# Side work at every fourth weight tile, and an early function table, in a mixture-of-experts loop

## The chip, the core and the metric

The kernel runs on one core of a Trainium2 chip. The core's engines run side by side and wait for one another by semaphores: TensorE (PE; its weight loads are shown apart as PEld), VectorE (DVE), ScalarE (ACT), GpSimd (POOL), and SyncE (SP), which here only issues transfers. Sixteen DMA engines move data. The metric is the device time of one execution in microseconds; lower is better.

## The reference

One transformer layer over 1024 tokens of width 1024: three kinds of attention side by side, an output projection, and a mixture of 32 experts, of which each token takes two; then a norm. The part that matters here is the mixture. Each expert's tokens go through two weight matrices (1024x1024 up, 512x1024 down); the result is scaled by the token's gate and added up per token:

```python
dest = pad_start[e_sorted] + jnp.arange(n_assign) - start[e_sorted]
buf = jnp.zeros((n_blocks * MOE_BLOCK, D), h.dtype).at[dest].set(h[tok_sorted])
...
def expert_block(args):
    xb, e = args
    g, u = jnp.split(xb @ w_up[e], 2, axis=-1)
    return (jax.nn.silu(g) * u) @ w_down[e]
...
y = y[dest] * gate.reshape(-1)[order][:, None].astype(h.dtype)
return jax.ops.segment_sum(y, tok_sorted, num_segments=n_tok)
```

## The kernel before, in words

The attention and the routing come first. The expert stage follows, some 650 us of the run. It gives each expert one block of 128 token slots. Tokens beyond an expert's 128 go to overflow blocks, which run in a second loop at the very end, under an If that is taken only where there are any.

**The main loop.** It walks 360 weight tiles of 128x1024 float32 (512 KB each) of 30 experts, eight tiles of the up matrix (kind 0) and four of the down matrix (kind 1) each. The down block of an expert stands behind the up block of the next one, so that twelve tiles make one expert's turn. The remaining two experts are done behind the loop, together with the final norm. For each tile j the loop writes, in this order:

- turns that are due (`e_turn`, line 1856): PE transposes of a 128x512 half of the next expert's gathered rows `xg` (the two halves at the second and third tile of a down block) or of the hidden rows `sg` (at the fifth tile of an up block) into a PSUM tile `ept`. ACT copies that tile out (`xh` or `ah`, line 1858), then DVE subtracts this from it (`xl` or `al`, line 1859), and the tile is free after that;
- `e_mm` (lines 1866 to 1868): six matmuls with the high and low pieces of tile j into `epu` (up) or `epy` (down);
- one step of the side work, if any is left;
- at the end of an up block `e_silu`: ACT's Silu and DVE's product (`sg`, lines 1872 and 1873);
- `split_next(j + 3)`: ACT rounds a later tile to `whi` (line 1840), DVE takes the rest `wlo` (line 1841); there are three such pairs of buffers. The raw buffer in the ring of 34 is then free, and SP issues the load of tile j + 37;
- at the end of a down block `e_scatter`: half of the scaled result `y` by ACT, half by DVE (line 1892), and POOL adds it to memory (line 1886).

The order on PE, DVE, ACT and POOL is that of the code (a manual schedule); the tile framework puts in the semaphores and picks a free buffer.

**The side work.** `overflow_tables` is a generator that builds the tables of the overflow blocks, about 60 steps of mostly one DVE instruction. It begins at tile 52. Its first 26 steps are small tables (lines 1740 to 1797). Then it takes a PSUM tile for itself, `ptab`, and from there on makes 16 pairs of one-hot matrices (`ohr` and `ohc`, lines 1809 and 1811, a step each) and adds their 16 products up in `ptab` on PE (line 1805), each product two pairs behind its matrices. A last pair of steps reads `ptab`. `ptab` comes from the pool that the turns use, under the same name, and that pool has two buffers of it:

```python
pe = Ex.enter_context(tc.tile_pool(name="pe", bufs=2, space=PSUM))
pt = pe.tile([128, 4, 128], F32, name="ept")      # in e_turn
ptab = pe.tile([128, 4, 128], F32, name="ept")    # in overflow_tables
```

**The start of the stage.** `gates()` computes the gates with two Exp on ACT (lines 1706 and 1710). Then the first expert's two halves are turned. POOL sets six small tiles `gxs` to zero ahead of it (line 2046). ACT can use a function only while the table that holds it is loaded; where the next function needs another table, an ACT_TABLE_LOAD stands ahead of it. Exp and Silu need different ones here; the copies do not.

Of the kernel before, what the change touches and what calls it, by code (L numbers as in the profile page):

```python
# [12 lines left out]
AF = mybir.ActivationFunctionType  # L13
# [53 lines left out]
def body(nc, tc, d, tap=None, upto=None):  # L67
# [1238 lines left out]
    class Til:  # L1306
# [5 lines left out]
        def small(self, name, shape, bufs=2):  # L1312
            return w2.tile([128] + shape, F32, name=name, bufs=bufs)
# [387 lines left out]
    def gates():  # L1701

        ge = rt_("ge", [NT, 4])
        V.tensor_tensor(ge, lg[:, :, 0:4], bc(gmx[:, :, 0], 4), op=OP.subtract)
        yield
        nc.scalar.activation(ge, ge, AF.Exp)
        dd = rt_("dd", [NT])
        V.tensor_sub(dd, gmx[:, :, 2], gmx[:, :, 1])
        yield
        nc.scalar.activation(dd, dd, AF.Exp)  # L1710
        pg = rt_("pg", [NT])
        V.tensor_reduce(pg, ge, axis=AX.X, op=OP.add)
        yield
        V.reciprocal(pg, pg)
        yield
        ds_ = rt_("ds", [NT])
        V.tensor_scalar(ds_, dd, 1.0, None, op0=OP.add)
        yield
        V.reciprocal(ds_, ds_)
        yield  # L1720
        V.tensor_mul(gate[:, 0, :], ds_, pg)
        yield
        V.tensor_mul(ds_, ds_, dd)
        yield
        V.tensor_mul(gate[:, 1, :], ds_, pg)
        yield
        gd = [rt_(f"gd{j}", [NT, E]) for j in range(2)]
        for j in range(2):
            V.tensor_tensor(gd[j], cio99[:, None, :].to_broadcast([128, NT, E]), bc(eid[:, j, :], E), op=OP.is_equal)
            yield  # L1730
            V.tensor_tensor(gd[j], gd[j], bc(gate[:, j, :], E), op=OP.mult)
            yield
        V.tensor_add(gd[0], gd[0], gd[1])
        nc.gpsimd.dma_start(GD.rearrange("(t p) e -> p t e", p=128), gd[0])
        yield
# [113 lines left out]
    def x_tiles():  # L1849
        return (e2.tile([128, 8, 128], F32R, name="xh", bufs=1), e2.tile([128, 8, 128], F32R, name="xl", bufs=1))  # L1850

    def e_turn(src, n, h, l, g):

        pt = pe.tile([128, 4, 128], F32, name="ept")
        for i in range(4):
            nc.tensor.transpose(pt[:, i, :], src[:, (4 * g + i) * 128:(4 * g + i + 1) * 128], ident)  # L1856
        gs = slice(4 * g, 4 * g + 4)
        nc.scalar.copy(h[:, gs, :], pt)  # L1858
        nc.vector.tensor_sub(l[:, gs, :], pt, h[:, gs, :].bitcast(F32))  # L1859

    def e_mm(ps, k, nk, w, a):
        hi, lo = w
        ah, al = a
        for n in range(2):
            cs = slice(512 * n, 512 * n + 512)
            nc.tensor.matmul(ps[:, cs], lhsT=ah[:, k, :], rhs=hi[:, cs], start=(k == 0), stop=False)  # L1866
            nc.tensor.matmul(ps[:, cs], lhsT=ah[:, k, :], rhs=lo[:, cs], start=False, stop=False)  # L1867
            nc.tensor.matmul(ps[:, cs], lhsT=al[:, k, :], rhs=hi[:, cs], start=False, stop=(k == nk - 1))  # L1868

    def e_silu(pu):  # L1870
        sg = e2.tile([128, 512], F32, name="sg", bufs=1)
        nc.scalar.activation(sg, pu[:, 0:512], AF.Silu)
        nc.vector.tensor_mul(sg, sg, pu[:, 512:])
        return sg

    def a_tiles():
        return (e2.tile([128, 4, 128], F32R, name="ah", bufs=1), e2.tile([128, 4, 128], F32R, name="al", bufs=1))
# [11 lines left out]
    def e_scatter(py, gi_, g_):  # L1889
        y = e2.tile([128, D], F32, name="y", bufs=2)  # L1890
        nc.scalar.activation(y[:, :HD], py[:, :HD], AF.Copy, scale=g_)
        V.scalar_tensor_tensor(y[:, HD:], py[:, HD:], g_, m5[:, HD:], op0=OP.mult, op1=OP.mult)  # L1892
        y_scatter(y, gi_)
# [19 lines left out]
    def split_next(j):  # L1913
        if j < NM:
            pieces[j] = split(loaded.pop(j))
            if j + RW < len(stream):
                load_tile(j + RW)
            else:
                fill()
# [24 lines left out]
    gxs = [small(f"gx{i}", [E]) for i in range(6)]  # L1944
# [6 lines left out]
    def gate_of(e):  # L1951
        return gxs[e % 6][:, e:e + 1]

    def gather(e):
        e_gather(gU[:, e:e + 1], xgs[e % 2])
        gate_rows(gU[:, e:e + 1], gxs[e % 6])
# [43 lines left out]
    def turn32(src, n, dst, g):  # L2000

        pt = pe.tile([128, 4, 128], F32, name="ept")
        for i in range(4):
            nc.tensor.transpose(pt[:, i, :], src[:, (4 * g + i) * 128:(4 * g + i + 1) * 128], ident)
        (nc.vector.tensor_copy if g else nc.scalar.copy)(dst[:, 4 * g:4 * g + 4, :], pt)
# [15 lines left out]
    with tc.manual_schedule(engines={ET.PE, ET.DVE, ET.Activation, ET.Pool}):  # L2021
# [24 lines left out]
            nc.gpsimd.memset(g_, 0.0)  # L2046
        for _ in gates():
            pass
        e_turn(xgs[0], 8, *xs[0], 0)
        e_turn(xgs[0], 8, *xs[0], 1)  # L2050
        for j in range(1, SP):
# [8 lines left out]
        side_work = iter(())  # L2060
        ps = None
        for j, (b, k) in enumerate(stream[:NM]):
            kind, e = blocks[b]
            for what, e_, g in extra.get(j, ()):
                if what == "h":
                    acts[e_] = a_tiles()
                    e_turn(sgs.pop(e_), 4, *acts[e_], 0)
                else:
                    if e_ >= ME:
                        if e_ == ME and g == 0:  # L2070
                            xs[ME], xs[E - 1] = (a.bitcast(F32) for a in x_tiles())
                        turn32(xgs[e_ % 2], 8, xs[e_], g)
                    else:
                        if g == 0:
                            xs[e_] = x_tiles()
                        e_turn(xgs[e_ % 2], 8, *xs[e_], g)
                    if g == 1 and e_ + 2 < E:
                        gather(e_ + 2)
            if k == 0:
                ps = (pe.tile([128, D], F32, name="epu"), None)[0] if kind == 0 else pd.tile([128, D], F32, name="epy")  # L2080
            e_mm(ps, k, (8, 4)[kind], pieces.pop(j), xs[e] if kind == 0 else acts[e])
            if (b, k) == (8, 0):
                side_work = overflow_tables(cid2)
            next(side_work, None)
            if kind == 0 and k == 7:
                sgs[e] = e_silu(ps)
            split_next(j + SP)
            if kind == 1 and k == 3:
                e_scatter(ps, gU[:, e:e + 1], gate_of(e))
# [283 lines left out]
```

## Time and profile before

| | us |
|---|---|
| median of 3 runs (1587.26 to 1592.28) | 1589.0 |
| the profiled execution, its own time | 1589.09 |
| its span, first to last instruction | 1587.3 |
| PE busy | 1447.1 (91%) |
| DVE busy | 1144.6 (72%) |
| ACT busy | 947.5 (60%) |

The profile comes from one execution. 1.8 us of its time lie outside the span. A share of busy time is an average over stages with different limits: in the expert loop PE, DVE and the DMA engines are each near their limit, in the stages before it they are not.

### The profile page before, as it was taken

What the parts mean: (1) busy time and instruction counts of PE and PEld (TensorE: products, weight loads), DVE (VectorE), ACT (ScalarE), POOL (GpSimd) and SP (SyncE); (2) the same over time, 40 slices, a digit from 0 to 9 for tenths busy, and PEclk for the clock granted to TensorE, in tenths of its full rate; (3) what the DMA queues carried; (4) which work ended last, traced back from release to release, by engine and by line L of the source; (5) the groups of instructions that cost most, each with busy time, mean ns of one, the idle gap of its engine ahead of it and who ended that gap; (6) DMA issues with size and microseconds to landing.
All of it is one profiled execution on the core that took longest, in us unless ns stands there. A gap on an engine that the chain in (4) does not pass through costs nothing. (4 is left out here: it accounts for less than half of the span.)

```text
span 1587.3 us, 24530 instructions
## 1 busy us (share of the span) xinstructions
PE 1447.1 (91%) x8577; PEld 1182.9 (75%) x8577; DVE 1144.6 (72%) x1929; ACT 947.5 (60%) x1544; POOL 486.9 (31%) x611
## 2 busy tenths in 40 slices
PE   6899799888999989699999859999999999999993
PEld 3699677767767867689999857877788888888751
DVE  6613655894545436586777768999999999999936
ACT  3523554773534441477766427877788888888721
POOL 0001333221313211347788653232222222222101
PEclk9999899999989979799999979999999999999997
DMA  9433563014554369522222678999999999999994
GB/s 333 142 88 117 163 223 119 21 48 144 132 134 111 74 222 300 212 74 67 87 67 67 246 269 320 363 348 343 335 371 369 357 364 358 364 354 363 360 333 158
DMA packets 166272, 354.11 MB, mean 223 GB/s; under 512 B 29407, under 2 KB 85194, under 8 KB 166144
## 3 DMA queue, kind: packets, MB, share of 16 engines
q1 hardware_dynamic: 139552, 305.68, 54.5%
q0 software_dynamic: 22992, 36.76, 9.0%
q10 hardware_dynamic: 3600, 10.06, 1.6%
q8 instruction: 68, 1.11, 0.3%
q14 instruction: 60, 0.49, 0.1%
HBM read 315.68 MB, written 55.72 MB: 234 GB/s over the span
## 5 line engine op out<-in xcount | busy, mean ns | idle before, releaser
L1841 DVE TENSOR_TENSOR wlo<-wraw,whi 128x1024 fp32r<-128x1024 f32 x360 | 435.7, 1221 | 31.7 <-ACT whi L1840 27.8
L1840 ACT CAST whi<-wraw 128x1024 fp32r<-128x1024 f32 x360 | 374.9, 1049 | 107.9 <-PE epu L1868 65.4
L1866 PE MATMUL epu<-whi,xh 128*128 128x512 f32 x480 | 195.0, 406 | 2.2 <-ACT xh L1858 2.2
L1867 PE MATMUL epu<-wlo,xh 128*128 128x512 f32 x480 | 191.8, 400 | 1.9 <-DVE wlo L1841 1.8
L1868 PE MATMUL epu<-whi,xl 128*128 128x512 f32 x480 | 190.1, 396 | 0.4 <-DVE xl L1859 0.4
L1270 DVE TENSOR_REDUCE nm<-S 128x1 f32<-128x1280 f32 x64 | 94.9, 1489 | 51.0 <-PE S L1269 43.3
L1845 POOL DMA_INDIRECT xg<-H,gidx x30 | 31.9, 1064 | 294.3 <-PE ept L1856 294.0
L377 PE MATMUL pj<-wh,hh 128*128 128x256 f32 (+1 forms) x384 | 113.8, 296 | 3.1 <-ACT kbT L333 3.1
L379 PE MATMUL pj<-wh,hl 128*128 128x256 f32 (+1 forms) x384 | 112.4, 293 | 0.0
L378 PE MATMUL pj<-wl,hh 128*128 128x256 f32 (+1 forms) x384 | 112.3, 292 | 0.0
L1867 PEld LDWEIGHTS epu<-wlo,xh 128*128 128x128 f32 x480 | 90.8, 189 | 28.1 <-DVE wlo L1841 9.6
L1866 PEld LDWEIGHTS epu<-whi,xh 128*128 128x128 f32 x480 | 90.9, 189 | 22.4 <-ACT xh L1858 2.7
L1868 PEld LDWEIGHTS epu<-whi,xl 128*128 128x128 f32 x480 | 90.7, 189 | 22.3 <-DVE xl L1859 1.3
L1886 POOL DMA_INDIRECT YS<-y,gidx x30 | 71.1, 2369 | 115.0 <-DVE y L1892 96.4
L1866 PE MATMUL epy<-whi,ah 128*128 128x512 f32 x240 | 101.1, 421 | 3.3 <-DVE y L1892 3.3
L366 PE MATMUL pj<-hh,wh 128*128 128x512 f32 (+1 forms) x240 | 99.7, 416 | 0.0
L1275 ACT ACTIVATE p<-S,nm 128x1280 f32<-128x1280 f32 x64 | 84.7, 1331 | 21.2 <-DVE nm L1270 21.2
L1867 PE MATMUL epy<-wlo,ah 128*128 128x512 f32 x240 | 95.3, 397 | 0.1
L1868 PE MATMUL epy<-whi,al 128*128 128x512 f32 x240 | 94.9, 395 | 0.0
L368 PE MATMUL pj<-hh,wl 128*128 128x512 f32 (+1 forms) x240 | 92.3, 385 | 0.0
L367 PE MATMUL pj<-hl,wh 128*128 128x512 f32 (+1 forms) x240 | 92.1, 384 | 0.0
L1268 PE MATMUL S<-ak,aq 128*128 128x512 f32 (+1 forms) x192 | 75.4, 393 | 10.8 <-ACT p L1275 10.0
(493 smaller groups left out, 3479.7 us busy)
## 6 DMA issues: line engine op xcount, KB each, us to landing
wraw<-w_up SPq DMA_DIRECT2D x254, 512.0 KB
wraw<-w_down SPq DMA_DIRECT2D x127, 512.0 KB
wm<-w_mod SPq DMA_DIRECT2D x32, 512.0 KB
raw<-w_in SPq DMA_DIRECT2D x22, 512.0 KB
wm<-w_mod SPq DMA_DIRECT2D x32, 256.0 KB
aq<-QS SPq DMA_DIRECT2D x64, 128.0 KB
ak<-KS SPq DMA_DIRECT2D x8, 640.0 KB
xn<-x SPq DMA_DIRECT2D x8, 512.0 KB
```

The lines of the kernel that those rows point to most:

```text
L366: nc.tensor.matmul(ps[:, :n], lhsT=a, rhs=x, start=(k == 0), stop=False)
L367: nc.tensor.matmul(ps[:, :n], lhsT=a, rhs=y, start=False, stop=False)
L368: nc.tensor.matmul(ps[:, :n], lhsT=b, rhs=x, start=False, stop=(k == 7))
L377: nc.tensor.matmul(ps[:, :n], lhsT=a, rhs=wh[:, k, :], start=(k == 0), stop=False)
L378: nc.tensor.matmul(ps[:, :n], lhsT=a, rhs=wl[:, k, :], start=False, stop=False)
L379: nc.tensor.matmul(ps[:, :n], lhsT=b, rhs=wh[:, k, :], start=False, stop=(k == 7))
L1270: V.tensor_reduce(u.nm[:, m:m + 1], sv, axis=AX.X, op=OP.max, negate=True)
L1840: nc.scalar.copy(hi, raw)
L1841: nc.vector.tensor_sub(lo, raw, hi.bitcast(F32))
L1866: nc.tensor.matmul(ps[:, cs], lhsT=ah[:, k, :], rhs=hi[:, cs], start=(k == 0), stop=False)
L1867: nc.tensor.matmul(ps[:, cs], lhsT=ah[:, k, :], rhs=lo[:, cs], start=False, stop=False)
L1868: nc.tensor.matmul(ps[:, cs], lhsT=al[:, k, :], rhs=hi[:, cs], start=False, stop=(k == nk - 1))
```

## The change

The side work advances at every fourth tile of the loop and not at every tile, and ACT runs a Silu over one column of zeros ahead of the first expert's turns.

```diff
         for _ in gates():
             pass
+
+        nc.scalar.activation(gxs[5][:, 0:1], gxs[5][:, 0:1], AF.Silu)
         e_turn(xgs[0], 8, *xs[0], 0)
         e_turn(xgs[0], 8, *xs[0], 1)
...
             e_mm(ps, k, (8, 4)[kind], pieces.pop(j), xs[e] if kind == 0 else acts[e])
             if (b, k) == (8, 0):
                 side_work = overflow_tables(cid2)
-            next(side_work, None)
+            if j % 4 == 0:
+                next(side_work, None)
```

On ACT the table load moves. Before, it stands ahead of the first expert's Silu (line 1872; `m` and `cid` are loads that ACT only issues):

```order
L1710 ACTIVATE dd<-dd 128x8 [waits DVE_49]
L1858 CAST xh<-ept 128x512 [waits PE_49] x2
L1840 CAST whi<-wraw 128x1024 x2
L2057 DMA m_9608<-MR 128x1024 [waits DMAHW5_49]
L2059 DMA cid_9765<-dest 128x16 [waits DMAHW7_49]
L1840 CAST whi<-wraw 128x1024 [waits PE_49,Activation_49]
L1840 CAST whi<-wraw 128x1024 [waits DVE_49,PE_49] x4
L1840 CAST whi<-wraw 128x1024 [waits DMAHW1_49,DVE_49,PE_49]
L1840 CAST whi<-wraw 128x1024 [waits DVE_49,PE_49]
L1872 ACT_TABLE_LOAD
L1872 ACTIVATE sg<-epu 128x512 [waits PE_49]
```

Now it stands behind the second Exp, with the new Silu, which waits for POOL's zeros, behind it:

```order
L1710 ACTIVATE dd<-dd 128x8 [waits DVE_49]
L2050 ACT_TABLE_LOAD
L2050 ACTIVATE gx_9616<-gx_9616 128x1 [waits Pool_49]
L1858 CAST xh<-ept 128x512 [waits PE_49] x2
L1840 CAST whi<-wraw 128x1024 x2
```

Behind these the row is that of before, without the load: none is left inside the first expert.

On PE the 16 products spread out. Before, they go from tile 82 to tile 110, one in two tiles; now from tile 172 to tile 284, one in eight. This is the down block of tiles 172 to 175 on PE, from the first half's turn (`xg`) to the second half's, before:

```order
L1868 MATMUL epy<-whi,al 128x512
L1856 MATMUL ept<-ident,xg_9610 128x128 [waits DMASW2_49,PE_49]
L1856 MATMUL ept<-ident,xg_9610 128x128 x3
L1866 MATMUL epy<-whi,ah 128x512 [waits Activation_49]
L1867 MATMUL epy<-wlo,ah 128x512 [waits DVE_49]
...
L1856 MATMUL ept<-ident,xg_9610 128x128 [waits PE_49]
```

and the same place now:

```order
L1868 MATMUL epy<-whi,al 128x512
L1805 MATMUL ept<-ohc,ohr 128x16 [waits PE_49]
L1856 MATMUL ept<-ident,xg_9610 128x128 [waits DMASW2_49,PE_49]
L1856 MATMUL ept<-ident,xg_9610 128x128 x3
L1866 MATMUL epy<-whi,ah 128x512 [waits Activation_49]
L1867 MATMUL epy<-wlo,ah 128x512 [waits DVE_49]
...
L1856 MATMUL ept<-ident,xg_9610 128x128 [waits DVE_49]
```

The second half's turn now waits for DVE. Between the first product and the last there are 10 such pairs of turns, at tiles 173/174, 185/186 and so on to 281/282, and the second turn of each carries this wait. Before, two pairs lie between the first product and the last (tiles 89/90 and 101/102), and their second turns carry it.

On DVE the row of a down block's first tiles, outside the side work, is this before (`sg` ends the up block ahead of it):

```order
L1873 TENSOR_TENSOR sg<-sg,epu 128x512
L1841 TENSOR_TENSOR wlo<-wraw,whi 128x1024 x2
L1859 TENSOR_TENSOR xl<-ept,xh 128x512
L1841 TENSOR_TENSOR wlo<-wraw,whi 128x1024
L1859 TENSOR_TENSOR xl<-ept,xh 128x512
```

Now, as long as the side work lasts, it is this:

```order
L1873 TENSOR_TENSOR sg<-sg,epu 128x512
L1841 TENSOR_TENSOR wlo<-wraw,whi 128x1024
L1809 TENSOR_SCALAR ohr<-iot,sl 128x128
L1841 TENSOR_TENSOR wlo<-wraw,whi 128x1024
L1859 TENSOR_TENSOR xl<-ept,xh 128x512
```

One step of the side work has come between the two `wlo` ahead of the first `xl`. The other two steps of an expert's twelve tiles stand behind `y` and behind `al`.

## Rows read from the trace of the kernel before

**Rows 1.** Busy time by stretch: PE, PEld, DVE, ACT, POOL, PEclk, DMA share, GB/s.

```profile
1025.00:1150.00 125.00, 120.22 (x564) 95.57 (x564) 119.09 (x168) 94.54 (x108) 33.74 (x20) 1.00 0.97 344
1275.00:1400.00 125.00, 125.00 (x580) 100.69 (x578) 119.26 (x119) 102.87 (x119) 31.29 (x21) 1.00 0.99 361
```

**Rows 2.** Timeline, POOL: start us, us, instruction; one scatter an expert.

```profile
1025.95 2.32 POOL L1886 DMA_INDIRECT YS<-y,gidx  x1 [3.19 <-DVE y L1892]
...
1084.07 2.53 POOL L1886 DMA_INDIRECT YS<-y,gidx  x1 [3.33 <-DVE ohr L1809]
...
1125.90 2.54 POOL L1886 DMA_INDIRECT YS<-y,gidx  x1 [3.47 <-DVE ohr L1809]
1145.11 2.34 POOL L1886 DMA_INDIRECT YS<-y,gidx  x1 [3.18 <-DVE y L1892]
...
1471.53 2.34 POOL L1886 DMA_INDIRECT YS<-y,gidx  x1 [3.18 <-DVE y L1892]
```

**Rows 3.** Timeline, PE, a down block outside the side work.

```profile
1479.75 0.39 PE L1866 MATMUL epy<-whi,ah 128*128 128x512 f32 x1
...
1480.22 0.39 PE L1868 MATMUL epy<-whi,al 128*128 128x512 f32 x1
...
1483.00 0.38 PE L1856 MATMUL ept<-ident,xg 128*128 128x128 f32 x2
```

**Rows 4.** Timeline, PE, a down block while `ptab` is held.

```profile
1092.93 0.39 PE L1866 MATMUL epy<-whi,ah 128*128 128x512 f32 x1
...
1097.91 0.66 PE L1856 MATMUL ept<-ident,xg 128*128 128x128 f32 x4 [1.41 <-DVE xl L1859]
...
1099.57 0.39 PE L1868 MATMUL epy<-whi,al 128*128 128x512 f32 x1
1099.80 0.29 PE L1805 MATMUL ept<-ohc,ohr 128*128 128x16 f32 x2
...
1100.26 0.39 PE L1867 MATMUL epy<-wlo,ah 128*128 128x512 f32 x1
```

**Rows 5.** Timeline, DVE, the block of rows 3.

```profile
1483.79 0.69 DVE L1859 TENSOR_TENSOR xl<-ept,xh 128x512 fp32r<-128x512 f32 x1
```

**Rows 6.** Waits, 1025 to 1150 us: engine and line, waited for, us, times, longest.

```profile
DVE oin L1753 <- POOL one__10647 L1751: 1.7, 1, 1.7
```

**Rows 7.** Waits, 1150 to 1500 us.

```profile
DVE wlo L1841 <- ACT whi L1840: 13.6, 76, 0.2
```

**Rows 8.** Timeline, ACT and PE, end of the first expert's up block.

```profile
962.66 1.28 ACT L1872 ACT_TABLE_LOAD   x1
963.95 0.60 ACT L1872 ACTIVATE sg<-epu 128x512 f32<-128x512 f32 x1
...
962.79 1.04 PE L1856 MATMUL ept<-ident,xg 128*128 128x128 f32 x8
966.02 0.53 PE L1866 MATMUL epu<-whi,xh 128*128 128x512 f32 x1 [2.20 <-ACT xh L1858]
...
967.40 0.79 PE L1868 MATMUL epu<-whi,xl 128*128 128x512 f32 x1 [0.43 <-DVE xl L1859]
...
969.70 0.43 PE L1867 MATMUL epu<-wlo,xh 128*128 128x512 f32 x1
```

**Rows 9.** Busy time by stretch, short ones; the granted clock is behind POOL's bracket.

```profile
966.00:968.00 2.00, 1.55 (x4) 0.80 (x4) 1.95 (x3) 0.46 (x1) 0.50 (x1) 0.59 1.04 414
...
1096.00:1098.00 2.00, 0.59 (x4) 0.16 (x3) 2.00 (x5) 1.14 (x2) 0.00 (x0) 1.00 1.00 360
```

**Rows 10.** Timeline, POOL and ACT, ahead of the first expert.

```profile
945.98 0.49 POOL L2046 MEMSET gx<- 128x32 f32 x6
...
949.42 0.59 ACT L1858 CAST xh<-ept 128x512 fp32r<-128x512 f32 x1 [6.75 <-PE ept L1856]
```

**Rows 11.** Timeline, POOL and SP, end of the loop: last scatter, and the loads behind it.

```profile
1518.43 1.56 POOL L1886 DMA_INDIRECT YS<-y,gidx  x1 [8.36 <-DVE both L1968]
...
1526.86 2.95 SPq L76 DMA_DIRECT2D wraw<-YS  x6
```

**Rows 12.** The scatters of 1000 to 1590 us, issue to landing.

```profile
DMA to landing us min/median/max: 8.1/9.9/10.7
```

## The prediction, made before the changed kernel ran

> **What bounds the kernel now.** I read busy time by stretch first. Behind the side work the loop is even: in 1275 to 1400 us PE is busy for all 125 us at full clock, DVE for 119, and the DMA engines at 0.99. In 1025 to 1150 us, where the side work runs, PE starts 564 matmuls in place of 580, and the DMA share is 0.97 [rows 1]. So the stretch is worth something, and PE sets the pace there. How much is read from POOL's scatters, one an expert. Outside the side work 18 of them span 1145.11 to 1471.53, 18.13 us each. With it, six span 1025.95 to 1145.11, 119.16 us in place of 108.8: the side work costs 10.4 us now [rows 2]. The first three of these six, with the small tables, lose 3.7 us (58.12 against 54.4); the next two, with the products, take 20.92 each and so lose 2.8 each [rows 2].
>
> Where the 2.8 go is the second thing to see. In an undisturbed down block PE begins the block at 1479.75 and the second half's turn at 1483.00, 3.25 us later [rows 3]. While `ptab` is held, the block begins at 1092.93 and that turn at 1097.91, 4.98 us later, 1.41 of it idle, ended by DVE's `xl` [rows 4]. With one of the two `ept` buffers kept by `ptab`, the second half must wait until DVE has read the first half out. In the undisturbed block the second turn is already running when `xl` of the first begins: 1483.00 against 1483.79 [rows 3, 5]. So DVE can't be on time for it, with side work or without: `xl` ends at 1484.48, 4.73 us behind the block's start. The wait hangs on how long `ptab` is held, not on how dense the steps are.
>
> **The change part by part.**
>
> *Removed.* All that the side work costs in its present place: −10.4 us. In it is DVE's wait of 1.7 us for POOL's `one_` [rows 6]; now the scan stands four tiles, some 6 us, behind that memset, and POOL, which runs the memset behind one scatter more, has time for it.
>
> *Added: the turns that wait.* The 16 products now go from tile 172 to tile 284, and ten pairs of turns lie between, where there were two. Price of one: by the starts, 4.98 − 3.25 = 1.73 us, with one product in it. By the period, 20.92 − 18.13 less the five other products is 1.7 (below). The side step that now stands ahead of the first `xl` is in these rows too, since one stands there in rows 4. I take 1.7 us, ten times: +17.0 us. It can't be hidden: PE has nothing else in its queue, behind the waiting turn stand the block's other matmuls, and behind these the next expert's. ACT and DVE wait for free `whi` and `wlo` meanwhile, SP issues loads later, and that costs nothing while PE is late itself. Bounds: 1.41, the idle time alone, and 1.9, if a step delays `xl` by its whole length: 14 to 19 us.
>
> *Added: the products.* From the matmul ahead of a product to the second one behind it PE takes 0.69 us (1099.57 to 1100.26) [rows 4], and 0.47 where there is none (1479.75 to 1480.22, the same two steps) [rows 3]: 0.22 each. Five of the 16 fall inside the pairs above, where they are counted. Eleven remain: +2.4 us.
>
> *Added: the 30 steps ahead of the first product, one in four tiles.* No row shows a lone step. Below, they cost nothing, since DVE waits for ACT 76 times in 350 us, 13.6 us in all, 0.18 each [rows 7], and most steps are as short. Above, they cost what they cost now, packed: 3.7 us, of which 1.7 is the wait on POOL. I take +2.0, as three kinds of 0.4 to 0.7 us don't fit.
>
> *Moved: the table load.* Before, ACT loads the table from 962.66 to 963.94, and Silu starts at 963.95. PE finished the up block at 962.79 and stands still for 2.20 us until `xh` [rows 8]. Without the load Silu follows PE's signal: up to 1.16 us earlier (963.95 − 962.79); I take 1.0 for the signal's way. At the new place ACT stands idle for 6.75 us until 949.42, and POOL's zeros, for which the new Silu waits, are there at 946.47 [rows 10]. Even a load that began only then would end 1.6 us ahead of `xh`, so nothing is queued behind it. There is a second gain: behind the 2.20 us of idle time the granted clock was 0.59 [rows 9], mostly the lower of its two levels (1.2 of 2.4 GHz), and five matmul starts from 967.40 to 969.70 took 2.30 us [rows 8] in place of 1.17 (five times half of 0.47). With 1.2 us of idle time the clock should stay, as it did behind 1.41 (1.00 in 1096 to 1098) [rows 9]: 1.1 us. Together −2.1 us, with bounds of −0.5 and −2.3.
>
> The Trainium skill (ScalarE: Activation LUTs, What ACT_TABLE_LOAD costs) gives 1283 ns for the load and 1380 ns more for a drain at each switch. The load's row agrees; of the drain the trace shows nothing, as Silu starts 0.01 us behind the load. With the drain counted the moved load would be worth 1.4 us more.
>
> *The tail.* Behind the loop the output's loads wait for the last scatter (1518.43 to 1526.86, 8.4 us) [rows 11]. With PE slower for ten experts the transfers have less behind them at the end, but the quickest scatter of the stage takes 8.1 us [rows 12]: −0.3, at most −1.5, if the loads land sooner too. Else the tail moves with the loop's end.
>
> Sum: −10.4 + 17.0 + 2.4 + 2.0 − 2.1 − 0.3 = +8.6 us. On the profiled execution's 1589.09 that is 1597.7. This execution lies 0.1 above the median of 1589.0, so I predict 1597.7 for the median.
>
> **The rivals.**
>
> *The turns' wait shrinks* (other side). DVE has fewer steps, so `xl` could come early enough. For it speaks that the two waits on record have three side steps around them. Against it speaks the undisturbed block, where `xl` ends 1.48 us behind the start of the second turn with no step near [rows 3, 5]. It decides at 0.84 us a pair ((17.0 − 8.6) / 10): below that the kernel is faster. With no wait at all PE would gain 8.4 us, but the DMA engines, at 0.97 in the stretch, have 0.03 x 125 = 4 us to give there [rows 1]. With the table's 2.1 that is about 1583.
>
> *The bounds fall together low*: pairs at 1.41, small steps hidden, 1.5 in the tail: −10.4 + 14.1 + 2.4 + 0 − 2.3 − 1.5 = +2.3, so 1591.4, no change that could be told.
>
> *The clock falls at the turns.* Where no product stands ahead of the pair, in five of the ten, PE would be idle for 1.6 us, between 1.41, behind which the clock held, and 2.20, behind which it fell [rows 4, 8, 9]. Each fall costs 1.1 us: 1597.7 + 5.5 = 1603, or 1609 for all ten. The Trainium skill (TensorE: Matmul & The Clock Gate, The HAM clock gate) has the clock follow how busy the array has been recently. No run here shows what an idle 1.6 us does.
>
> *The load's move does nothing*, because the second Exp or another function takes the table back: 1599.8. The order on ACT speaks against it, as no second load stands there.
>
> **How the numbers follow.** The forecast, 1593.8 to 1601, has 0.62; the low bounds 0.17; the falling clock 0.13; the vanishing wait 0.05; the idle move 0.03. A measurement here tells 0.3%, 4.8 us, from no change. Slower is the forecast, the clock and the idle move: 0.78; same 0.16; faster 0.06. The range reaches to the low bounds' time and into the falling clock's: 1591 to 1605.
>
> **What the profile would show.** Ten waits of PE's turns for DVE's `xl`, 1.4 to 1.6 us idle each; scatters some 20.1 us apart for ten experts, and 18.2 to 18.5 in the ten turns ahead of these; no table load at 962, and PE idle for about 1.2 us there with the clock at 1.00; DMA share well below 0.99 in the held stretch. I am wrong if the scatters stay at 18.2 while `ptab` is held, or if the clock shows under 1.00 in that stretch.

## The result, and the profile after

The changed kernel takes 1599.4 us in the median against 1589.0: a ratio of 1.0071, 95% interval 1.0048 to 1.0094, so 7.6 to 14.9 us slower. The profiled execution of after took 1595.66 us, 3.7 below its median, with a span of 1593.8 us.

The stretches of [rows 1] first (PE, PEld, DVE, ACT, POOL busy, then granted clock, DMA share and GB/s):

```profile
1025.00:1150.00 125.00, 124.28 (x572) 99.16 (x571) 120.21 (x135) 101.60 (x117) 35.22 (x21) 1.00 1.00 367
1275.00:1400.00 125.00, 115.79 (x538) 91.52 (x537) 111.09 (x125) 93.29 (x107) 34.38 (x18) 1.00 0.97 341
```

The loss has moved: the stretch that lost 4.8 us of PE's time before has nearly all of it back, and the one that was full is 9 us short, at a clock of 1.00. How long that lasts is read from POOL's scatters, as in [rows 2] (start, duration, instruction):

```profile
1022.08 2.32 POOL L1886 DMA_INDIRECT YS<-y,gidx  x1 [3.18 <-DVE y L1892]
...
1205.52 2.53 POOL L1886 DMA_INDIRECT YS<-y,gidx  x1 [2.98 <-DVE ohr L1809]
1225.65 4.81 POOL L1886 DMA_INDIRECT YS<-y,gidx  x1 [3.44 <-DVE ohc L1811]
1246.03 2.54 POOL L1886 DMA_INDIRECT YS<-y,gidx  x1 [3.47 <-DVE ohr L1809]
...
1408.08 2.42 POOL L1886 DMA_INDIRECT YS<-y,gidx  x1 [3.47 <-DVE sido L1813]
```

From 1205.52 to 1408.08 lie ten periods of 20.26 us, alternately 20.14 and 20.37; the ten ahead of them, with the small tables, take 183.44 us, 2.2 above ten undisturbed ones of 18.125. The place of the ten long ones is that of [rows 3, 4], a down block with `ptab` held (PE's timeline):

```profile
1234.29 0.40 PE L1866 MATMUL epy<-whi,ah 128*128 128x512 f32 x1
...
1239.27 0.66 PE L1856 MATMUL ept<-ident,xg 128*128 128x128 f32 x4 [1.58 <-DVE xl L1859]
```

and the waits of 1205 to 1408 us (us, times, longest):

```profile
PE ept L1856 <- DVE xl L1859: 14.9, 10, 1.6
```

From the start of the block to the second turn it takes 4.98 us, as in [rows 4], here without a product between. There are ten such waits, 1.5 us each in the mean.

The other part of the change shows at the first expert, [rows 8, 9]. Here are ACT's timeline, PE's, and the clock by stretch (behind POOL's bracket):

```profile
939.22 1.28 ACT L2050 ACT_TABLE_LOAD   x1
...
943.04 0.20 ACT L2050 ACTIVATE gx<-gx 128x1 f32<-128x1 f32 x1 [2.53 <-POOL gx L2046]
...
959.68 0.60 ACT L1872 ACTIVATE sg<-epu 128x512 f32<-128x512 f32 x1 [0.36 <-PE epu L1868]
...
959.48 1.04 PE L1856 MATMUL ept<-ident,xg 128*128 128x128 f32 x8
961.75 0.50 PE L1866 MATMUL epu<-whi,xh 128*128 128x512 f32 x1 [1.23 <-ACT xh L1858]
...
963.12 0.79 PE L1868 MATMUL epu<-whi,xl 128*128 128x512 f32 x1 [0.65 <-DVE xl L1859]
...
962.00:964.00 2.00, 1.35 (x4) 0.83 (x4) 1.67 (x3) 0.19 (x1) 1.17 (x1) 0.75 1.01 406
964.00:966.00 2.00, 2.00 (x6) 1.51 (x6) 0.00 (x0) 0.77 (x1) 0.00 (x0) 0.50 1.04 402
```

The load stands far ahead of the first expert now, and PE's idle time is 1.23 us in place of 2.20. But the clock fell to 0.50 all the same. From the start of the turns at the up block's end (959.48 here, 962.79 before) to the first scatter it takes 26.3 us in place of 26.9, a gain of 0.6.

The tail, as in [rows 11]:

```profile
1526.24 1.56 POOL L1886 DMA_INDIRECT YS<-y,gidx  x1 [6.72 <-DVE both L1968]
...
1532.76 3.79 SPq L76 DMA_DIRECT2D wraw<-YS  x8
```

From scatter to load it is 6.5 us, in place of 8.4, and SP issues the eight loads in 3.8 us. From the last scatter to the span's end it is 67.6 us, 1.3 less than before.

Between the two profiled executions, the loop from the first scatter to the 28th (of 30) gains or loses as follows: 10.6 us of side work removed, 2.2 added by the small steps, 21.7 by the held stretch (ten periods, and 0.4 in the one behind), together +13.3. Add −0.6 at the first expert, −1.6 in the last period (the clock, see the end), −1.3 in the tail and −3.3 ahead of the first expert's turns, in stages that the change leaves as they were: +6.5, the difference of the spans.

### The profile page after: what moved, and what is told of

Read it like the earlier page. It is cut to its first block, busy times and chain, and to the rows that moved or that the text cites. A ratio compares the mean times of both kernels' runs of the same rounds, so it can differ in the third digit from the quotient of the medians.

```text
span 1593.8 us, 24530 instructions
## 1 busy us (share of the span) xinstructions
PE 1445.8 (91%) x8577; PEld 1180.3 (74%) x8577; DVE 1145.7 (72%) x1929; ACT 947.9 (59%) x1545; POOL 502.8 (32%) x611
## 5 line engine op out<-in xcount | busy, mean ns | idle before, releaser
L1886 POOL DMA_INDIRECT YS<-y,gidx x30 | 86.9, 2898 | 113.6 <-DVE y L1892 54.0
L1275 ACT ACTIVATE p<-S,nm 128x1280 f32<-128x1280 f32 x64 | 84.6, 1331 | 20.8 <-DMA hT<-MR 15.0
L1268 PE MATMUL S<-ak,aq 128*128 128x512 f32 (+1 forms) x192 | 76.0, 396 | 10.4 <-ACT p L1275 9.6
```

## The experiments

My theory: what costs is `ptab`'s buffer, kept over ten pairs of turns, and each pair costs 1.6 us. The rival: the spread itself costs, by steps between the splits or by products in ten experts in place of three. The stages ahead differ by several us from one execution to the next (the first turns start between 935 and 949 us in these profiles), so beside the times I read the time from the first scatter to the 28th, over 27 undisturbed periods of 18.125 us. It was 10.6 us before and is 24.0 after.

**e1_table: the early Silu alone.** The line behind `gates()` stays; the step's condition goes:

```
-            if j % 4 == 0:
-                next(side_work, None)
+            next(side_work, None)
```

> The early Silu alone, with one step of the side work at every tile, as before the change. By the prediction's step the table's move is worth 2.1 us (1.0 for the load, 1.1 for the clock), so 1586.9. By what the trace of after shows, where the clock fell to 0.50 in 964 to 966 us although PE had stood idle for only 1.23 us, it is worth 0.6, so 1588.4. The profile tells them apart better than the time: granted clock at the first expert, and the time from its turns to expert 0's scatter (26.9 us before, 26.3 after).

Measured: 0.9991 (0.9970 to 1.0013). The loop is that of before (10.5 us). Turns to first scatter take 26.4 us, and the clock fell. So the gain is the smaller one of the two expected, though the time alone can't tell it from none.

**e2_fourth: the step at every fourth tile alone.**

```
-        nc.scalar.activation(gxs[5][:, 0:1], gxs[5][:, 0:1], AF.Silu)
```

> The step at every fourth tile alone, with the table load where it was. Theory (ten pairs of turns wait because ptab keeps one of two ept buffers): ten periods of 20.2 us between scatters, and 1600 us, 0.6 above the whole change; by the prediction's price of the table it would be 1601.5. A table load at 962 us again and 2.2 us of idle time on PE behind it.

Measured: 1.0077 (1.0050 to 1.0105), 24.0 us in the loop, periods of 20.13 to 20.36. So the step's condition is the whole loss. The first expert was a surprise. The load stands in its old place again (ACT, PE, clock):

```profile
961.25 1.28 ACT L1872 ACT_TABLE_LOAD   x1
...
964.61 0.50 PE L1866 MATMUL epu<-whi,xh 128*128 128x512 f32 x1 [2.20 <-ACT xh L1858]
...
965.98 0.50 PE L1868 MATMUL epu<-whi,xl 128*128 128x512 f32 x1 [0.64 <-DVE xl L1859]
...
964.00:966.00 2.00, 0.75 (x3) 0.32 (x3) 1.90 (x3) 1.05 (x3) 1.70 (x2) 1.00 1.03 403
```

PE is idle for the same 2.20 us as in [rows 8], and the clock stays at 1.00, in 966 to 968 us too. Turns to scatter take 25.8 us, less than in after. So the length of the idle time doesn't decide whether the clock falls here.

**e6_hold: the buffer held, and nothing else.** The kernel before, with the last step (the last two products and the reading of `ptab`) put off:

```
-            next(side_work, None)
+            if j < 110 or j >= 206:
+                next(side_work, None)
```

> The kernel before (a step at every tile, the table load where it was), but the last step, which runs the last two products and reads ptab, waits until tile 206, so that ptab keeps its buffer over ten pairs of turns with no steps between. Theory (the held buffer): eight more waits of 1.4 to 1.6 us, periods of 19.6 to 19.8 us with nothing else in them, +12 to +14 us: 1601 to 1603. Rival (not the buffer, but the steps and products spread over ten experts): the eight periods stay at 18.13 and the time at 1589.

Measured: 1.0079 (1.0048 to 1.0109), 12.5 us slower, 23.5 in the loop. POOL's scatters:

```profile
1183.19 2.35 POOL L1886 DMA_INDIRECT YS<-y,gidx  x1 [3.45 <-DVE y L1892]
1202.93 2.35 POOL L1886 DMA_INDIRECT YS<-y,gidx  x1 [3.46 <-DVE y L1892]
```

With no step and no product in it a period takes 19.74 us: 1.62 for the buffer alone. The rival falls as the main cause: seven such periods make 11.3 of the 12.8 us by which this loop is longer than before. PE's timeline between these two scatters, and a little beyond, shows a pair of turns with no step of the side work near it:

```profile
1191.40 0.40 PE L1866 MATMUL epy<-whi,ah 128*128 128x512 f32 x1
...
1196.18 0.66 PE L1856 MATMUL ept<-ident,xg 128*128 128x128 f32 x4 [1.38 <-DVE xl L1859]
...
1205.11 0.60 PE L1856 MATMUL ept<-ident,sg 128*128 128x128 f32 x4
```

From the start of the block to the second turn it takes 4.78 us here, and 4.98 in after and in [rows 4], where a step stands ahead of the first `xl`. From there to the turn of the hidden rows (`sg`) it takes 8.93 us.

**e4_groups: no accumulator held over a turn.** All else as in the change:

```
-        ptab = pe.tile([128, 4, 128], F32, name="ept")
+        acc = rt_("acc", [NOV])
+        for n_ in range(0, 2 * NT, 4):
...
+            ptf = pe.tile([128, 4, 128], F32, name="ept").rearrange("p a b -> p (a b)")[:, :NOV]
+            for m_ in hot:
+                nc.tensor.matmul(ptf, lhsT=hot[m_][0], rhs=hot[m_][1], start=(m_ == n_), stop=(m_ == n_ + 3))
+            if n_ == 0:
+                V.tensor_scalar(acc, ptf, 8192.0, None, op0=OP.add)
+            else:
+                V.tensor_add(sido if n_ + 4 == 2 * NT else acc, ptf, acc)
+            yield
...
-            if j % 4 == 0:
+            if j in turns:
```

`turns` holds the tiles 52, 56, ... 152, and then, for four experts, eight for one-hots and one for the group of products, behind the first matmuls of an up block.

> The whole change, but no accumulator is held over a turn: the 16 products run in four groups of four, each into an ept tile of its own behind the first matmuls of an up block, and VectorE adds the group into a small SBUF tile. The small tables' steps stay at every fourth tile. Theory (the held buffer): no wait of the turns for xl, four periods with 0.9 us more for four products each, the small steps at 2.1, the table at 0.6: -10.4 + 2.1 + 3.5 - 0.6 = -5.4, so 1583.6, less what the DMA engines, at 0.97 to 1.00, keep back. Rival (the spread of steps over more experts itself costs, by the steps on VectorE between the splits): the periods stay at 19.5 to 20 us for four experts and the time is 1588 or more.

Measured: 0.9974 (0.9949 to 0.9999), −4.1 us; the loop 5.4 us above undisturbed, 5.3 less than before. PE's timeline shows the pair and the group:

```profile
1238.16 0.60 PE L1859 MATMUL ept<-ident,xg 128*128 128x128 f32 x4
...
1239.99 0.60 PE L1859 MATMUL ept<-ident,xg 128*128 128x128 f32 x4
...
1244.62 0.74 PE L1812 MATMUL ept<-ohc,ohr 128*128 128x16 f32 x6
1245.20 0.38 PE L1812 MATMUL ept<-ohc,gd 128*128 128x16 f32 x2
```

The second turn follows the first after 1.83 us without a wait. The four periods with products take 18.83 to 18.98 us, together 3.25 above undisturbed ones: 0.20 for each of the 16, with the one-hots around them counted in.

**e3_second, e5_fifth: other densities.** `j % 2 == 0` and `j % 5 == 0`.

> The whole change with a step at every second tile. ptab is then kept over five pairs of turns. Theory (the held buffer: 1.61 us for each pair, as with the buffer held and nothing else, and 0.22 for each product): five periods of 20.4 us (three products in each), small steps at 2 to 3 us, in sum 2 to 4 us above the kernel before, and 6 to 8 below the change with every fourth tile. Rival (the spread itself costs or pays): the periods stay at 20.2 to 20.3, as many as fit, or the losses don't go with the number of pairs.

> The whole change with a step at every fifth tile: the products lie in tiles 202 to 342, with twelve pairs of turns between. Theory: twelve periods of 20.0 to 20.2 us, 2 to 4 us above every fourth tile, though the steps are sparser. Rival (sparser steps are cheaper): below every fourth tile.

Measured: every second tile 1.0002 (0.9981 to 1.0023), the loop at 12.9 us with five periods of 20.14 to 20.37, which is 2.3 above before and inside the forecast, though the time alone doesn't show it; every fifth tile 1.0048 (1.0025 to 1.0071), 23.6 us and 0.4 more in the 28th period, with twelve long periods, 20.01 in the mean. The number of long periods came as foreseen in both. The forecast for every fifth tile, 2 to 4 us above the change, fell: twelve pairs cost no more than ten. Twelve times 1.62 and 14 products inside are 22.2 us, 12 periods of 1.88 are 22.6; but the small steps cost 1.0 us here, not 2.2, and the side steps among the turns less than in after. So the place of a step within an expert's twelve tiles counts, and at every fifth tile it changes from expert to expert: from the start of the block to the second turn it is 4.97 or 4.98 us at the three pairs with a step ahead of the first `xl`, and 4.70 to 4.79 at the other nine.

**e7_dense_products: sparse small tables, dense products.** `if j % 4 == 0 or j > 152:`

> The whole change, but from tile 153 on a step at every tile: the small tables are sparse, the one-hots and products as dense as before the change. ptab is kept over two or three pairs. Theory: two periods of 20.9 us and one of 19, small steps 2.1, no wait for POOL: 2 to 3 us below the kernel before. Rival (the spread of the small tables is what costs): above the kernel before.

Measured: 0.9980 (0.9960 to 1.0001), the loop 9.7 us; three long periods of 20.3 to 20.8, where I had forecast two of 20.9 and one of 19. The loop gains 0.9 us on before. The forecast gain of 2 to 3 us lies inside the interval of the time, and so does none. The sparse small tables pay a little, and the longer third period takes part of it back.

**e8_groups_eighth: e4 with a small step at every eighth tile.** `set(range(52, 260, 8))`, the groups behind it.

> The kernel with four groups of products and no held accumulator, its small tables' steps at every eighth tile in place of every fourth. In the run with every fourth tile four periods of 18.52 to 18.70 us hold the larger steps of the tables and lose 1.8 us together. Theory: VectorE has some 0.07 us to spare for each tile, and four tiles aren't enough to hide a step of 0.4 to 0.7 us, but eight nearly are; the small steps then cost 0.5 to 1 us in place of 2.1, and the loop is 1 to 1.6 us shorter than with every fourth tile, 6 to 7 us below the kernel before. Rival: each step costs what it costs, however sparse, and the four losses become eight of half the size.

Measured: 0.9947 (0.9928 to 0.9966), but the loop is at 5.0 us, 0.3 below e4, not 1.0 to 1.6. The theory of VectorE's spare time fell. Three periods of 18.53 or 18.54 remain, and in each of them one of the long steps stands behind tile 4, ahead of the first `xl` with one `wlo` between; VectorE's timeline in one of them:

```profile
1139.35 0.68 DVE L1763 TENSOR_TENSOR be<-oin,iot 128x512 f32<-128x512 f32 x1
...
1141.09 0.68 DVE L1862 TENSOR_TENSOR xl<-ept,xh 128x512 fp32r<-128x512 f32 x1
```

**e9_groups_phase, e10_fourth_shifted: the steps two tiles later.** In e9 `range(54, 158, 4)` for the small steps and the one-hots moved off tile 4; in e10, on the whole change:

```
-            if j % 4 == 0:
+            if j % 4 == 2:
```

> The kernel with four groups of products and no held accumulator, with the small tables' steps at every fourth tile again, but two tiles later: behind tiles 2, 6 and 10 of an expert's twelve in place of 0, 4 and 8, and the one-hots behind tiles 7, 9 to 11 and 0 to 3, none behind tile 4. Theory (a step behind tile 4 stands ahead of xl of the first half on VectorE and costs its length; elsewhere most of a step is hidden): no period above 18.3 us outside the groups, the loop's first 27 periods together 493.0 to 493.8 us (494.7 with steps at 0, 4, 8; 494.4 with every eighth tile), 1577 to 1582. Rival (each step costs its length wherever it stands): periods of 18.5 us as before, 494.4 to 494.8.

> The whole change with the steps two tiles later (behind tiles 2, 6 and 10 of an expert's twelve in place of 0, 4 and 8): ptab is kept over ten pairs of turns as before, but no side step stands ahead of xl. Theory: the held periods fall from 20.26 us to 20.1 (18.13, 1.61 for the wait, 0.35 for 1.6 products), the small steps from 2.1 to 0.5 or 1, in sum 2.5 to 3.5 us below the change and still 7 to 10 above the kernel before. Rival (the step's place doesn't matter): 20.26 and 2.1 as in the change.

Measured: e9 0.9945 (0.9923 to 0.9968), its first 27 periods 493.10 us, within the forecast. One period of 18.49 remains, with the step `be` (0.68 us) in it, where none above 18.3 was forecast. For e10 it is 1.0015 (1.0000 to 1.0030), the loop at 18.5 us, 5.4 below the change. Its held periods:

```profile
1223.06 2.34 POOL L1886 DMA_INDIRECT YS<-y,gidx  x1 [3.40 <-DVE y L1892]
1243.04 2.34 POOL L1886 DMA_INDIRECT YS<-y,gidx  x1 [3.44 <-DVE y L1892]
...
1403.50 2.34 POOL L1886 DMA_INDIRECT YS<-y,gidx  x1 [3.45 <-DVE y L1892]
```

They take 20.05 us in the mean and the small steps some 0.6 us, both as foreseen; but there are nine and not ten, since the first product, two tiles later, comes behind the first of the ten pairs, and so the loop gains more than the 2.5 to 3.5 forecast. From the start of the block to the second turn it takes 4.78 or 4.79 us, as in e6. The time was forecast wrong, +2.4 us and not 7 to 10: the loop's +7.9 stands there, but the first expert takes 24.9 us in this profile (load gone, clock at full), 2.0 less than before, and the tail 65.6, 3.3 less.

e9 and e8 beat both kernels, by 8.7 and 8.4 us against before; between the two the times don't decide, and by the loop e9 is 1.3 us ahead.

## Why the prediction was right, step by step

The median lies 1.7 us above the forecast, inside its range, and the mechanism of the main term is the one foretold: it is shown by e6 (the buffer alone costs 1.62 us a pair) and e4 (without the held buffer the wait is gone).

- *Removed, −10.4.* Right: the loop of before stands 10.6 above undisturbed.
- *The turns that wait and their products, +17.0 and +2.4.* The number, ten, and the wait, 1.4 to 1.6 us, are right; the size was 2.3 too low (21.7). The forecast says that the side step ahead of the first `xl` is in its rows already, and that holds: 4.98 us from block start to second turn in [rows 4] and at all ten pairs of after, 4.78 without the step (e6, e10). But the price of 1.7 was too low. Over the whole period a pair costs 1.62 (e6) and the step 0.20 more, 1.82 in all, which makes 1.2 us in ten. The step behind `y` was put at nothing. Here are PE's second turn and the turn of the hidden rows behind it, at the first held pair of after:

```profile
1218.91 0.66 PE L1856 MATMUL ept<-ident,xg 128*128 128x128 f32 x4 [1.41 <-DVE xl L1859]
...
1228.03 0.60 PE L1856 MATMUL ept<-ident,sg 128*128 128x128 f32 x4
```

  They lie 9.12 us apart with no product between, and 8.93 in e6, where no step stands behind `y`. Behind five of the ten pairs it is so; behind the other five a product stands there, and the 9.11 to 9.14 us (9.35 behind the last, with two products) leave nothing for the step. So 18.2 for the ten pairs, 1.2 for six steps behind `y` (the sixth in the period ahead of the first pair) and 2.2 for the eleven other products make 21.6 of the 21.7. The same prices hold for the dense rows: 18.13, 1.82 and five products of 0.20 are 20.95, against the 20.92 of [rows 2]. That it is the step behind `y` that costs the 0.19 is read from its place, not shown by a run that moves it alone.
- *The small steps, +2.0.* Right: 2.2. That they cost this by where they stand (0.6 two tiles later, 1.0 at every fifth tile) I had not seen.
- *The table load, −2.1.* Measured: −0.6. The load's own 1.0 is exact: with the clock at full, turns to first scatter take 25.81 us with the load (e2) and 24.83 to 24.86 without (e5, e8, e9, e10). The other 1.1, "the clock should stay", failed: without the load it fell in after, e1, e3, e4 and e7 (26.33 to 26.39, e4 26.41) and not in the other four; with it, it fell before and in e6, not in e2. The length of the idle time was no ground to expect either outcome. By the Trainium skill (ScalarE: Activation LUTs, What ACT_TABLE_LOAD costs) a drain would add 1.4 us to a switch; the 0.97 measured leaves no room for it.
- *The tail, −0.3.* Too little: 1.3 in after's profile, and 2.3 to 3.3 in e2, e5, e6 and e10, where PE was late as well. The 8.1 us that the forecast took as the least that a scatter needs were no floor: the loads start 6.1 to 6.8 us behind the start of the last scatter in those five profiles. Where the loop is fast the tail is longer: 69 to 71 us in e1, e3, e4, e8 and e9 (e7, with 66.9, is the exception). SP's waits at the weights' loads show what goes along with it, in after and then in e9 (us, times, longest):

```profile
SPq L1911 <- DVE wlo L1841: 298.3, 268, 10.8
...
SPq L1911 <- DMA wraw<-w_up: 72.9, 77, 2.8
```

```profile
SPq L1914 <- DMA wraw<-w_up: 212.6, 177, 3.5
...
SPq L1914 <- DVE wlo L1844: 105.3, 119, 9.7
```

In after SP mostly waits for a buffer that the split has to leave, so the loads are on time; in e9 it mostly waits for earlier transfers, and the output's loads have these ahead of them. That this is the cause of the tail's length is argued from these rows, not shown by a run that changes it alone.

The errors do not cancel: the forecast has 2.3 too little for the turns and 1.5 too much gain for the table, both on the same side, and against them 1.0 too little for the tail's gain. With the parts as measured (−10.6, +2.2, +21.7, −0.6, −1.3) the sum is +11.4, 2.8 above the forecast; the medians differ by 10.4. That the median came as near as 1.7 us is in part luck.

*The signs:* the ten waits and the missing load came as foretold. The long periods are 20.26 us in the mean, not 20.1, the clock at the first expert fell, and the DMA share in the held stretch is 0.97, hardly below the 0.99 of before. *The rivals:* the wait did not shrink; the clock stayed at 1.00 at all ten turns, behind 1.4 to 1.6 us of idle time; the load's move gained 0.6 us, and 2.0 where the clock stayed (e10).

## What to carry to other kernels

Ask of a step that is spread out not only what it costs, but what it holds meanwhile: an accumulator taken from a double-buffered pool turns every other user of the same tile name into a single-buffered one for as long as it lives, and that price goes by uses, not by steps. Short groups, added up in a small tile of their own, gave the spread without the price (e4). When steps are put between an engine's regular work, their place within the period can count more than their number: two tiles' shift took 1.6 us off the loop (e4 to e9), half the density 0.3 (e4 to e8). Part of what a loop gains can be given back behind it, here, as I read the rows but have not shown, because the transfers are then the ones that are late.

## What the runs showed of the hardware

The granted clock fell at the first expert in seven of the twelve profiles and stayed in five, and not by the idle time: behind 2.20 us it fell to 0.59 before and held 1.00 in e2, behind 1.23 it fell in after and held in e9. A fall cost 1.1 to 2.8 us with the load in place and 1.5 without. At the loop's end PE is idle for 3.3 us in every profile; in after the clock held 1.00 behind it and the last period took 8.3 us, in the profile of before the clock fell to 0.50 and the period took 9.9. In e9 the clock held 1.00 as well, but POOL's last scatter started later behind `y`, and the period took 9.7. In the other nine the clock fell. So one execution's clock at a place says little of the next one's, and I would now give a gain from a clock that stays as a chance, not as a term.
